# Three pieces of a gated macaron block's feed-forward stages put at other places: one split, one difference, one turning of a tile

## The chip, the cores and the metric

The kernel runs on one core of a Trainium2 chip. The metric is the device time of one execution in microseconds (us). Three timed runs of the kernel before gave 1066.24, 1067.35 and 1068.38 us; their median is 1067.35 us.

In the profile, PE is TensorE's matrix multiplication and PEld its loading of the stationary operand, DVE is VectorE, ACT is ScalarE, POOL is GpSimd, and SP is the engine that issues most of the DMAs.

## The reference, cut to what matters

One layer on 512 tokens of width 1024, all in float32:

```python
def rms_norm(x, g):
    return x * lax.rsqrt(jnp.mean(x * x, axis=-1, keepdims=True) + RMS_EPS) * g

def swiglu(h, w1, w3, w2):
    return (jax.nn.silu(h @ w1) * (h @ w3)) @ w2

x = x + 0.5 * swiglu(rms_norm(x, ffn1_norm), ffn1_w1, ffn1_w3, ffn1_w2)   # first FFN, inner width 2816
h = rms_norm(x, mix_norm); p = h @ w_in                                    # RWKV-7 and forgetting attention
x = x + (gate_a * y_a + gate_b * y_b) @ w_out                              # "the scan" and its projections
x = x + 0.5 * swiglu(rms_norm(x, ffn2_norm), ffn2_w1, ffn2_w3, ffn2_w2)    # second FFN
out = rms_norm(x, final_norm)
```

The change touches the two feed-forward stages (FFNs) alone; the mixers between them stay as they are.

## The kernel before, in words

**Every float32 product is three matmuls.** An operand is split into a rounded high part (`hi`) and the remainder (`lo = x - hi`), and hi·hi, hi·lo and lo·hi are added up in PSUM (`mm3`, lines 174 to 177; L175 to L177 in the profile, or L103 where the recorded queue below is in use). The high part is a cast by ACT, the low part a subtraction by DVE (`split`, `split_w`).

**Who sets the order.** From `written(True)` on, PE, DVE and ACT each run their instructions in the order in which the Python code names them (class `Queued`, lines 92 to 105: each call is issued behind the one before it on that engine). All of these instructions carry line 103 in the profile, so they are told apart by their tiles. Between engines only data counts: an instruction waits for what it reads and for the space it overwrites.

**The head of an FFN.** The first two feature tiles (128 of the 2816 inner features each) are done before the blocks, as plain products: `unit` multiplies a tile's split weights (`whi`, `wlo`) by the eight unnormalized input tiles, 24 matmuls, into the banks `pa` and `pb`. There are four such units: two weights (w1, w3) by two tiles. The weights of the fourth unit are split by `split_w(raws[3], KD, P)`. Meanwhile `normal` multiplies the eight input tiles in place by gain and 1/rms (tile `xS`, DVE); the blocks' sums and differences read these.

**The blocks.** The remaining 20 feature tiles of w1 and w3 are five blocks of four. A block takes seven products instead of eight (Strassen's scheme in Winograd's form), each of 24 matmuls into two banks. Class `Wide` lists the 35 products in `s.order` as (block, product): positions 0 to 3 are (0,0) (1,0) (0,6) (1,6), then come (0,1) (0,2) (0,4) (0,5) (1,1) (0,3) (1,2) (1,4) (1,5) (2,0) (1,3) and so on up to position 34. `blocks` walks this list: for each position and each of its two halves h it names the matmuls, at h = 1 the `finish` of the product (copies out of the banks, sums, gates), and after each half the split of the weights for the position two further on (`weight(m + 2, h)`).

A block's gate (silu of one product times another) leaves a tile `u` with tokens in the partitions, and the down projection needs features there. For early blocks a DMA does that turning: `apart` (two ACT copies of `u` into `p` or `sa`, as 16-bit words, and two transposing DMAs issued by SP) and later `joined` (four ACT copies from the turned words to the hidden tiles `rl` and `rh`). `joined` is entered in the table `joins` under the position at which it is to run. The last block's gate is turned by PE itself (`turn`: transposes `P<-ident,u`), behind steps 0, 2 and 3 of the next stage.

**The down projection.** Class `Seven` is seven products of 66 matmuls (11 steps k, two banks, three matmuls). `put(n, k, f, ...)` enters work behind step k of product n. `second`, `one` and `two` prepare its operands from the hidden tiles; `two(1)` is one subtraction of 128x1024 elements, written to the space of the old input tile (`xT<-rl` in the first FFN, `xS<-rl` in the second).

Of the kernel before, what the change touches and what calls it, by code (L numbers as in the profile page):

```python
# [19 lines left out]
P = 128  # L20
T = 512
D = 1024
KD = D // P
# [59 lines left out]
def kernel(  # L83
# [80 lines left out]
    def split_w(raw, kt, n, eng=None, hi_eng=None):  # L164
        hi = wp.tile([P, kt, n], F32R, tag="whi", name="whi", bufs=2)
        lo = wp.tile([P, kt, n], F32R, tag="wlo", name="wlo", bufs=2)
        (hi_eng or act).copy(hi[:], raw[:])  # L167
        (eng or dve).tensor_tensor(lo[:], raw[:], hi[:].bitcast(F32), op=ALU.subtract)  # L168
        return hi, lo
# [334 lines left out]
    class Seven:  # L504
# [65 lines left out]
        def run(s):  # L570
            tc.keep_in_program_order(act.preload_act_table_set("natural_log_exp_and_others"))
            X, Y, Z, V = s.banks

            def mm(ps, n, i, k, fresh, cols=slice(0, T)):
                qh, ql = [t[:, k % 4, i * P:(i + 1) * P] for t in s.q[n % 2][k // 4]]
                wh, wl = [t[:, k % 2, cols] for t in s.slots[k // 2]]
                stop = k == (9 if n == 6 else KH - 1)
                part = cols.stop - cols.start < T
                if part:
                    fresh = ps is Z  # L580
                else:
                    fresh, stop = fresh and k == 0, stop or n == 6 and k == 5
                return mm3(ps[i][:, cols], qh, ql, wh, wl, fresh and (not part or k == 8), stop, n in (2, 4, 5) or part and ps is V or n == 6 and k > 7)

            after = {}

            def put(n, k, *what):
                after.setdefault((n + k // KH, k % KH), []).append(what)

            put(0, 0, s.wide.turn, (1, 3), 0)  # L590
            put(0, 2, s.wide.turn, (0, 2), 1)
            put(0, 3, s.wide.turn, (1, 3), 1)
            put(0, 6, s.second, 2)
            put(0, 7, s.two, 2)
            for g, (two, four) in enumerate(((17, 25), (20, 28), (24, 31))):
                put(0, two, s.four, g)
                put(0, four, s.three, g)
            for n in range(6):
                for g in range(6):
                    put(n, min(2 * g + (5 if n == 0 else 3), 11 if n == 5 else 99), s.weight, n + 1, g)  # L600
                for g in range(3):
                    if n + 2 < 7:
                        put(n, min(4 * g + 3, 10) + (4 if n == 0 else 0), s.operand, n + 2, g)
            for n, ps in enumerate((X, Y, X, Z, Y, X)):
                for k in range(KH):
                    for i in range(2):
                        mm(ps, n, i, k, n in (0, 1, 3))
                    for f, *a in after.get((n, k), ()):
                        f(*a)
                for i in range(2):  # L610
                    for b, cols, by in (((0, LO, 0.5),), ((2, HI, 0.5),), ((0, HI, -0.5),), ((2, LO, 0.5),),
                                        ((0, HI, 0.5),), ((2, HI, -0.5), (2, LO, 0.5)))[n]:
                        s.out(ps[i][:], b + i, cols, by)
                if n == 0:
                    written(False)
                s.done(n)
            first_k, last_k = (0, 1, 2, 3, 6, 7, 10), (4, 5, 8, 9)
            for at, k in enumerate(first_k):
                for i in range(2):
                    s.mm = mm(V, 6, i, k, True)  # L620
                for f, *a in after.get((6, k), ()):
                    f(*a)
                s.between(at)
            for i in range(2):
                a, c = s.parts if i else (LO, None)
                for k in last_k:
                    s.mm = mm(V, 6, i, k, True, LO if c is None or k < 8 else a)
                    s.ending(i, k)
                s.out(V[i][:, a], i, a, 0.5)
                if c:  # L630
                    s.out(V[i][:, c], i, c, 0.5)
                    for k in last_k[2:]:
                        mm(Z, 6, i, k, k == 8, c)
                    s.out(Z[i][:, c], i, c, 0.5)
                    s.finished(i, a)
                s.finished(i, c or a)
# [13 lines left out]
    class Wide:  # L650
# [258 lines left out]
        def blocks(s, pa, pb, more):  # L909
# [12 lines left out]
                    (1, 2): ((s.low, 6),),  # L922
                    (2, 5): ((sv.second, 0),), (3, 2): ((sv.two, 0),),
                    (end, 0): ((sv.operand, 0, 0),), (end, 2): ((sv.operand, 0, 1),), (end, 6): ((sv.one, 0),),
                    (end, 5): ((sv.second, 1), (sv.one, 1)), (end, 4): ((sv.two, 1), *[(s.plain, sv.O[i], s.residual[i]) for i in range(2)])}
            for at, steps in more.items():
                todo[at] = tuple(todo.get(at, ())) + steps
            joins = {}
            for m, (b, n) in enumerate(s.order):
                apart = n == 4 and (b < EARLY or b == end)  # L930
                early = m < 2 * EARLY
                ps = s.X[b % 2] if n in (0, 2, 3, 5) or early else s.X[(b + 1) % 2] if n == 6 or apart else s.Y[b % 2]
                onto = n in (2, 3, 5) or (n == 6 and early) or (n == 4 and not apart)
                last = m + 2 >= len(s.order)
                if last:
                    sv.slots += s.ring[2 * m % 4:2 * m % 4 + 2]
                for h in range(2):
                    wh, wl = s.ring[(2 * m + h) % 4]
                    for i in range(2):
                        for k in range(2):  # L940
                            c = slice(i * P, (i + 1) * P)
                            if early:
                                qh, ql = [t[4 * (n > 0) + 2 * h + k][:, c] for t in raw]
                            else:
                                qh, ql = [t[:, 2 * h + k, c] for t in s.q[n]]
                            mm3(ps[i][:], qh, ql, wh[:, k], wl[:, k], not onto and h + k == 0, h + k == 2, onto)
                    if (b, n, h) == (end, 2, 0):
                        s.turn_half(b - 1)
                    if h == 1:
                        if m == len(s.order) - 1:  # L950
                            s.turns = dict(zip((0, 2, 1, 3), s.Y[end % 2] + s.X[1 - end % 2]))
                            act.activation(s.sa[0], ps[0][:], AF.Silu)
                            act.activation(s.sa[1], ps[1][:], AF.Silu)
                            s.turn((0, 2), 0)
                            for i in range(2):
                                dve.tensor_tensor(s.u[1][:, i], s.u[1][:, i], s.sa[i], op=ALU.mult)
                            sv.operand(0, 2)
                        else:
                            s.finish(m)
                    if h == 1:  # L960
                        for f, *a in soon.get((b, n), ()):
                            f(*a)
                    if not last:
                        s.weight(m + 2, h)
                    elif len(sv.slots) == 2:
                        sv.weight(0, h)
                    elif h == 0:
                        sv.slots.insert(2, s.last)
                        sv.weight(0, 2)
                        sv.weight(0, 3)  # L970
                    else:
                        sv.weight(0, 4)
                    if (m, h) in joins:
                        s.joined(*joins[m, h])
                    if b in (2, 3) and (n, h) == (1, 1):
                        s.apart(b - 1, 1)
                        joins[m + 3, 0] = b - 1, 1
                if n == 4 and b < end or (b, n) == (0, 3):
                    s.apart(b, int(n == 3))
                    joins[m + 3, 0] = b, int(n == 3)  # L980
                s.gate(m)
                for f, *a in todo.get((b, n), ()):
                    f(*a)
# [125 lines left out]
    with ExitStack() as mx:  # L1109
# [397 lines left out]
        at = b1.go(range(2))  # L1507
# [685 lines left out]
    with tc.tile_pool(name="hp", bufs=1) as hp:  # L2193
# [17 lines left out]
        wide.places()  # L2211
        wide.normal(range(2))
        wide.weight(0, 0)
        for m in range(2, KD):
            wide.unit(ps[1], ws[1], (m - 2,))
            wide.normal((m,))
        wide.unit(ps[1], ws[1], range(KD - 2, KD))
        pa, pb = bank("pa", pr), bank("pb", pf)
        ws.append(split_w(raws[3], KD, P))
        wide.unit(pa, ws[2])  # L2220
        wide.unit(pb, ws[3])
        wide.weight(0, 1)
# [30 lines left out]
```

## Time and profile before

| | |
|---|---|
| median of three runs | 1067.35 us (1066.24 to 1068.38) |
| the profiled execution's own time | 1067.36 us |
| its span, first to last instruction | 1065.7 us, granted TensorE clock 0.999 |
| PE busy | 1054.2 us, 99% of the span |
| first FFN, blocks | from about 32 to 224 us |
| second FFN, head / blocks / down projection | from about 738 / 760 / 952 us |

1067.36 - 1065.7 = 1.7 us lie outside the span. A matmul of 512 columns is shown as 0.39 us long, but matmuls overlap: they start about 0.227 us apart when nothing is waited for. So a wait of PE is read from the distance between two starts rather than from the "idle before" of a row. In the timeline a row is: start, duration, engine, line, operation, what it writes<-reads, shape and count, and in brackets the engine's idle time before it with what ended it; where "x2" or more stands, equal instructions that follow each other are merged and the duration is that of all of them.

### The profile page before, as it was taken

What the parts mean: (1) busy time and instruction counts of PE and PEld (TensorE: products, weight loads), DVE (VectorE), ACT (ScalarE), POOL (GpSimd) and SP (SyncE); (2) the same over time, 40 slices, a digit from 0 to 9 for tenths busy, and PEclk for the clock granted to TensorE, in tenths of its full rate; (3) what the DMA queues carried; (4) which work ended last, traced back from release to release, by engine and by line L of the source; (5) the groups of instructions that cost most, each with busy time, mean ns of one, the idle gap of its engine ahead of it and who ended that gap; (6) DMA issues with size and microseconds to landing.
All of it is one profiled execution on the core that took longest, in us unless ns stands there. A gap on an engine that the chain in (4) does not pass through costs nothing.

```text
span 1065.7 us, 16736 instructions
## 1 busy us (share of the span) xinstructions
PE 1054.2 (99%) x6178; PEld 862.5 (81%) x6178; DVE 841.4 (79%) x1171; ACT 712.4 (67%) x1107; POOL 242.4 (23%) x291
## 2 busy tenths in 40 slices
PE   9999999999999999999999999999999999999997
PEld 7888888888887887888777877888888888888886
DVE  7997776789865698878988878866698766699874
ACT  6777767776555766445888766544578868676554
POOL 1221220134203202312012230135311212114210
PEclk9999999999999999999999999999999999999999
DMA  7999999889946443443345574666989999979972
GB/s 215 262 193 233 230 196 253 201 194 189 230 125 170 116 112 97 129 132 106 85 82 117 130 186 154 196 160 166 282 199 212 208 229 231 212 205 202 235 187 80
DMA packets 194960, 190.25 MB, mean 179 GB/s; under 512 B 64958, under 2 KB 131070, under 8 KB 194878
## 3 DMA queue, kind: packets, MB, share of 16 engines
q1 hardware_dynamic: 147230, 110.78, 37.0%
q0 software_dynamic: 33392, 70.14, 34.8%
q10 hardware_dynamic: 14256, 8.26, 2.9%
q8 instruction: 49, 0.80, 0.3%
q14 instruction: 33, 0.27, 0.1%
HBM read 163.51 MB, written 12.52 MB: 165 GB/s over the span
## 4 chain that ended last, share of the span: by engine, by line
PE 88%; DVE 5%; ACT 3%; issue 2%; DMA 1%; SPq 1%; DVEq 0%; ACTq 0%
PE P L103 33%; PE P L177 6%; PE P L176 6%; PE P L175 6%; PE pgt L103 5%; PE spot L103 3%; PE pq L103 3%; PE l L103 2%; PE ppj L103 2%; PE pk L175 2%; PE pk L177 2%; PE pk L176 2%; PE pw L176 1%; PE pw L175 1%; PE pw L177 1%
## 5 line engine op out<-in xcount | busy, mean ns | idle before, releaser
L103 PE MATMUL P<-sraw,q 128*128 128x512 f32 x344 | 91.3, 389 | 0.0
L103 PEld LDWEIGHTS P<-sraw,q 128*128 128x128 f32 x344 | 64.6, 188 | 13.4
L103 PE MATMUL P<-swhi,q 128*128 128x512 f32 x224 | 71.2, 389 | 0.0
L167 ACT CAST whi<-raw 128x1024 fp32r<-128x1024 f32 (+2 forms) x42 | 40.4, 961 | 44.2 <-issue 14.1
L103 PE MATMUL P<-sraw,wxh 128*128 128x512 f32 x200 | 67.7, 390 | 0.0
L693 POOL DMA_DIRECT2D cb<-in_ffn_w_dram x20 | 24.1, 1207 | 143.3 <-DVE cd L103 76.2
L168 DVE TENSOR_TENSOR wlo<-raw,whi 128x1024 fp32r<-128x1024 f32 (+2 forms) x43 | 48.5, 1127 | 10.3 <-ACT whi L167 9.1
L103 PE MATMUL P<-swhi,wxh 128*128 128x512 f32 x144 | 56.6, 393 | 0.0
L103 PE MATMUL P<-swhi,wxl 128*128 128x512 f32 x144 | 56.1, 390 | 0.0
L103 PE MATMUL P<-swlo,wxh 128*128 128x512 f32 x144 | 56.1, 389 | 0.0
L693 POOL DMA_DIRECT2D cd<-in_ffn_w_dram x24 | 29.3, 1221 | 113.2 <-DVE sraw L103 59.7
L103 PE MATMUL P<-sraw,wxl 128*128 128x512 f32 x136 | 52.9, 389 | 0.0
L103 PEld LDWEIGHTS P<-swhi,q 128*128 128x128 f32 x224 | 42.0, 188 | 8.8
L103 ACT COPY RD<-spot 32x128 f32<-32x128 f32 (+2 forms) x128 | 39.9, 312 | 10.8 <-PE spot L103 8.8
L103 DVE TENSOR_TENSOR u<-P,u 128x512 f32<-128x512 f32 x52 | 33.4, 683 | 13.7 <-ACT u L103 13.7
L103 PEld LDWEIGHTS P<-sraw,wxh 128*128 128x128 f32 x200 | 37.5, 188 | 7.7
L103 PE MATMUL P<-swlo,q 128*128 128x512 f32 x112 | 43.6, 389 | 0.0
L552 POOL DMA_DIRECT2D ca<-in_ffn_w_dram x16 | 19.3, 1205 | 95.0 <-DVE swlo L103 65.6
L177 PE MATMUL pk<-xh,wlo 128*128 128x512 f32 x96 | 37.5, 392 | 1.0 <-DVE wlo L168 1.0
L175 PE MATMUL pk<-xh,whi 128*128 128x512 f32 x96 | 38.0, 396 | 0.4 <-DVE u L1257 0.4
L176 PE MATMUL pk<-xl,whi 128*128 128x512 f32 x96 | 37.5, 390 | 0.0
L177 PE MATMUL P<-swhi,wxl 128*128 128x512 f32 x96 | 37.3, 389 | 0.0
(632 smaller groups left out, 3441.9 us busy)
## 6 DMA issues: line engine op xcount, KB each, us to landing
cc<-in_ffn_w_dram SPq DMA_DIRECT2D x36, 512.0 KB
cb<-in_ffn_w_dram POOLq DMA_DIRECT2D x36, 512.0 KB, 6.6
cb<-in_ffn_w_dram SPq DMA_DIRECT2D x32, 512.0 KB
cd<-in_ffn_w_dram POOLq DMA_DIRECT2D x32, 512.0 KB, 8.1
ca<-in_ffn_w_dram POOLq DMA_DIRECT2D x32, 512.0 KB, 8.6
raw<-in_w_in_dram SPq DMA_DIRECT2D x27, 512.0 KB
ca<-in_ffn_w_dram SPq DMA_DIRECT2D x20, 512.0 KB
cd<-in_ffn_w_dram SPq DMA_DIRECT2D x18, 512.0 KB
```

The costliest lines, as they stand in the source:

```text
L103: q.last = do(*a, **kw)
L167: (hi_eng or act).copy(hi[:], raw[:])
L168: (eng or dve).tensor_tensor(lo[:], raw[:], hi[:].bitcast(F32), op=ALU.subtract)
L175: pe.matmul(ps, whi, xhi, start=first, stop=False, skip_group_check=onto)
L176: pe.matmul(ps, whi, xlo, start=False, stop=False, skip_group_check=onto)
L177: return pe.matmul(ps, wlo, xhi, start=False, stop=last, skip_group_check=onto)
L552: nc.gpsimd.dma_start(s.sum[g], src, accum_op=ALU.add)
L693: nc.gpsimd.dma_start(to, s.block(b, n, h), accum_op=ALU.add)
```

## The change

Three pieces move; no instruction is added or removed.

1. In both FFNs, the turning of block 0's first gate half, `apart(0, 0)`, moves from behind product (0,4) (position 6) to the middle of (0,5) (position 7), behind that half's `weight`. The `joined(0, 0)` that belongs to it moves from the middle of position 9 to the middle of position 10.
2. In both FFNs, `two(1)` moves from behind product (4,4), the last but one, to behind step 5 of the down projection's first product.
3. In the second FFN's head, the split of the fourth unit's weights moves ahead of the normalization of input tiles 2 to 7. The interleaving of `unit` and `normal` in the code goes too; as PE and DVE each keep their own order, that changes nothing on PE.

```diff
@@ Seven.run
             put(0, 3, s.wide.turn, (1, 3), 1)
+            put(0, 5, s.two, 1)
             put(0, 6, s.second, 2)
@@ Wide.blocks
-                    (end, 5): ((sv.second, 1), (sv.one, 1)), (end, 4): ((sv.two, 1), *[(s.plain, sv.O[i], s.residual[i]) for i in range(2)])}
+                    (end, 5): ((sv.second, 1), (sv.one, 1)), (end, 4): [(s.plain, sv.O[i], s.residual[i]) for i in range(2)]}
...
                     if (m, h) in joins:
                         s.joined(*joins[m, h])
+                    if m > 0 and (s.order[m - 1], h) == ((0, 4), 0):
+                        s.apart(0, 0)
+                        joins[m + 3, 0] = 0, 0
...
-                if n == 4 and b < end or (b, n) == (0, 3):
+                if n == 4 and 0 < b < end or (b, n) == (0, 3):
                     s.apart(b, int(n == 3))
                     joins[m + 3, 0] = b, int(n == 3)
@@ the second FFN
         wide.normal(range(2))
         wide.weight(0, 0)
-        for m in range(2, KD):
-            wide.unit(ps[1], ws[1], (m - 2,))
-            wide.normal((m,))
-        wide.unit(ps[1], ws[1], range(KD - 2, KD))
+        wide.unit(ps[1], ws[1])
+        ws.append(split_w(raws[3], KD, P))
+        wide.normal(range(2, KD))
         pa, pb = bank("pa", pr), bank("pb", pf)
-        ws.append(split_w(raws[3], KD, P))
         wide.unit(pa, ws[2])
         wide.unit(pb, ws[3])
```

On the engines this reads as follows. The order of PE's and SP's instructions is the same before and after; POOL's differs in one place of the second FFN's head, where a DMA issue and two copies change places.

DVE at the second FFN's head, before (`xS` with `rstd`: the normalizations; `wlo<-raw,whi`: splits of unit weights; `sraw`, `extra`, `swlo`: splits for the first block products):

```order
L103 TENSOR_TENSOR wlo<-raw,whi 128x1024 x2
L103 SCALAR_TENSOR_TENSOR xS_6333<-xS_6333,par,rstd 128x512 x2
L103 TENSOR_TENSOR sraw<-cd_6889,sraw 128x1024
L103 SCALAR_TENSOR_TENSOR xS_6333<-xS_6333,par,rstd 128x512 x2
L103 SCALAR_TENSOR_TENSOR xS_6334<-xS_6334,par,rstd 128x512 x4
L103 TENSOR_TENSOR wlo<-raw,whi 128x1024
L103 TENSOR_TENSOR extra<-cd_6890,sraw 128x1024
```

and now:

```order
L103 TENSOR_TENSOR wlo<-raw,whi 128x1024 x2
L103 SCALAR_TENSOR_TENSOR xS_6333<-xS_6333,par,rstd 128x512 x2
L103 TENSOR_TENSOR sraw<-cd_6889,sraw 128x1024
L103 TENSOR_TENSOR wlo<-raw,whi 128x1024
L103 SCALAR_TENSOR_TENSOR xS_6333<-xS_6333,par,rstd 128x512 x2
L103 SCALAR_TENSOR_TENSOR xS_6334<-xS_6334,par,rstd 128x512 x4
L103 TENSOR_TENSOR extra<-cd_6890,sraw 128x1024
```

The last `wlo` went from behind six normalizations to ahead of them.

DVE where the second FFN's blocks end and its down projection begins, before (`xS<-rl` is `two(1)`; `u<-u,sa` is the last block's gate, which PE turns; the others are splits):

```order
L103 TENSOR_TENSOR swlo<-ca_6888,swhi 128x1024
L103 TENSOR_TENSOR xS_6333<-rl_6882 128x1024
L103 TENSOR_TENSOR q_6899<-cb_6891,q_6899 128x1024
L103 TENSOR_TENSOR sraw<-cb_6892,sraw 128x1024
L103 TENSOR_TENSOR u_6897<-u_6897,sa_6974 128x512
L103 TENSOR_TENSOR u_6897<-u_6897,sa_6975 128x512
L103 TENSOR_TENSOR wxl_7118<-rl_6883,wxh_7117 128x768
L103 TENSOR_TENSOR extra<-cd_6889,sraw 128x1024
L103 TENSOR_TENSOR g_8401<-cd_6890,g_8400 128x512
L103 TENSOR_TENSOR swlo<-ca_6887,swhi 128x1024
```

and now:

```order
L103 TENSOR_TENSOR swlo<-ca_6888,swhi 128x1024
L103 TENSOR_TENSOR q_6899<-cb_6891,q_6899 128x1024
L103 TENSOR_TENSOR sraw<-cb_6892,sraw 128x1024
L103 TENSOR_TENSOR u_6897<-u_6897,sa_6974 128x512
L103 TENSOR_TENSOR u_6897<-u_6897,sa_6975 128x512
L103 TENSOR_TENSOR wxl_7118<-rl_6883,wxh_7117 128x768
L103 TENSOR_TENSOR extra<-cd_6889,sraw 128x1024
L103 TENSOR_TENSOR g_8400<-cd_6890,g_8399 128x512
L103 TENSOR_TENSOR xS_6333<-rl_6882 128x1024
L103 TENSOR_TENSOR swlo<-ca_6887,swhi 128x1024
```

`two(1)` went seven rows down; the two gate rows each stand one row higher. The first FFN has the same rows with `xT` for `xS`.

ACT from the middle of product (0,3) (position 9) to that of (1,2) (position 10) in the second FFN, before (`rl<-u`, `rh<-u`: the four copies of `joined(0, 0)`; `sa<-P`: the silu of (0,3); `sa<-u`: the copies of `apart(0, 1)`; the last two rows are the copies out of the banks of (1,2)):

```order
L103 COPY rl_6881<-u_6896 128x512
L103 COPY rh_6884<-u_6896 128x512
L103 COPY rl_6881<-u_6896 128x512
L103 COPY rh_6884<-u_6896 128x512
L103 ACTIVATE sa_6974<-P_7099 128x512
L103 ACTIVATE sa_6975<-P_7100 128x512
L103 CAST swhi<-cc_6894 128x1024
L103 COPY sa_6974<-u_6897 128x1024
L103 COPY sa_6975<-u_6897 128x1024
L103 CAST wxh_7117<-xS_6334 128x1024
L103 CAST sraw<-cb_6891 128x1024
L103 COPY u_6896<-P_7101 128x512
```

and now:

```order
L103 ACTIVATE sa_6974<-P_7099 128x512
L103 ACTIVATE sa_6975<-P_7100 128x512
L103 CAST swhi<-cc_6894 128x1024
L103 COPY sa_6974<-u_6897 128x1024
L103 COPY sa_6975<-u_6897 128x1024
L103 CAST wxh_7117<-xS_6334 128x1024
L103 CAST sraw<-cb_6891 128x1024
L103 COPY rl_6881<-u_6896 128x512
L103 COPY rh_6884<-u_6896 128x512
L103 COPY rl_6881<-u_6896 128x512
L103 COPY rh_6884<-u_6896 128x512
L103 COPY u_6896<-P_7101 128x512
```

The four copies went from ahead of the silu of (0,3) to just ahead of the copies out of the banks of (1,2). Earlier in the same list the two copies `p<-u` of `apart(0, 0)` changed places with one cast, `swhi<-cd`, and the first FFN's ACT list has the same moves.

More of the change, by code (lines that the diff above doesn't have):

```diff
@@ L924, in blocks @@
                     (end, 0): ((sv.operand, 0, 0),), (end, 2): ((sv.operand, 0, 1),), (end, 6): ((sv.one, 0),),
-                    (end, 5): ((sv.second, 1), (sv.one, 1)), (end, 4): ((sv.two, 1), *[(s.plain, sv.O[i], s.residual[i]) for i in range(2)])}
+                    (end, 5): ((sv.second, 1), (sv.one, 1)), (end, 4): [(s.plain, sv.O[i], s.residual[i]) for i in range(2)]}
             for at, steps in more.items():
-                todo[at] = tuple(todo.get(at, ())) + steps
+                todo[at] = tuple(todo.get(at, ())) + tuple(steps)
             joins = {}
```

## The prediction

> **What bounds the kernel now.** I read the page's busy times first, then busy time by stretch, then the chain of waits, and last the timeline around each edit.
>
> ```profile
> PE 1054.2 (99%) x6178; PEld 862.5 (81%) x6178; DVE 841.4 (79%) x1171; ACT 712.4 (67%) x1107; POOL 242.4 (23%) x291
> PE 88%; DVE 5%; ACT 3%; issue 2%; DMA 1%; SPq 1%; DVEq 0%; ACTq 0%
> core 0: us, PE busy (x) PEld busy (x) DVE busy (x) ACT busy (x) POOL busy (x), PEclk, DMA share, GB/s
> 65.20:114.10 48.90, 48.90 (x217) 40.52 (x216) 40.59 (x44) 38.49 (x50) 8.47 (x7) 1.00 0.99 223
> 793.30:842.20 48.90, 48.90 (x217) 40.51 (x216) 40.25 (x44) 38.54 (x50) 8.47 (x7) 1.00 0.99 221
> ```
>
> PE is the bound: 99% of the span, 88% of the chain. The two stretches are block positions 6 to 14 of the first and of the second FFN, where the first edit lies: nine products, 216 matmuls in 48.90 us, 0.226 us from start to start, with PE busy in all of the time. So there is no wait of PE to remove there, and one product takes 48.90 / 9 = 5.43 us. Whatever the change gains has to be a wait of PE elsewhere. The chain shows where DVE work of the moved kind stands ahead of PE:
>
> ```profile
> 754.06 1.15 DVE wlo L103
> 755.25 5.29 PE pb L103 x22
> ...
> 952.92 1.15 DVE xS L103
> ...
> 956.25 1.29 DVE u L103 x2
> 957.58 11.95 PE P L103 x55
> ```
>
> PE's fourth unit waits for the last weights' split (third edit), and PE's turning waits for a gate that stands behind `two(1)` on DVE (second edit).
>
> **Third edit, the head of the second FFN.** PE, then DVE, then ACT:
>
> ```profile
> 754.62 0.39 PE L103 MATMUL pb<-xl,whi 128*128 128x512 f32 x1
> 755.25 0.50 PE L103 MATMUL pb<-xh,wlo 128*128 128x512 f32 x1 [0.24 <-DVE wlo L103]
> ...
> 755.82 0.40 PE L103 MATMUL pb<-xl,whi 128*128 128x512 f32 x1
> ```
>
> ```profile
> 750.00 4.06 DVE L103 SCALAR_TENSOR_TENSOR xS<-xS,par,rstd 128x512 f32<-128x512 f32 x6
> 753.97 1.22 DVE L103 TENSOR_TENSOR wlo<-raw,whi 128x1024 fp32r<-128x1024 f32 x1
> 756.31 1.23 DVE L103 TENSOR_TENSOR extra<-cd,sraw 128x1024 fp32r<-128x1024 f32 x1 [1.12 <-ACT sraw L103]
> ...
> 765.78 1.22 DVE L103 TENSOR_TENSOR rl<-xS,xS 128x1024 f32<-128x1024 f32 x1
> ```
>
> ```profile
> 748.92 1.06 ACT L103 CAST whi<-raw 128x1024 fp32r<-128x1024 f32 x1 [0.16 <-PE pb L103]
> 755.23 1.05 ACT L103 CAST sraw<-cd 128x1024 fp32r<-128x1024 f32 x1 [5.25 <-DVE wlo L103]
> ```
>
> From 754.62 to 755.82 are three steps, 1.20 us where 3 x 0.227 = 0.68 would do: PE loses 0.52 us. The split's high part is ready at 748.92 + 1.06 = 749.98, which is when the six normalizations start at 750.00. Put first, the split ends at about 750.00 + 1.22 = 751.2, and its matmul would come at 754.62 + 0.23 = 754.85: 3.6 us of cover, the wait goes whole. Now the six normalizations are late, by one split's spacing, 1.14 us. Their first reader is the difference `rl<-xS,xS` at 765.78; they end at 755.2, so 10 us cover them. The second split of the first block weights (`extra`) waited for ACT, and ACT for the raw tile that `wlo` reads; both come some 1.1 us earlier or at the same time. Gain 0.52 us; the bounds are 0 (the wait passes to something equally late, of which I see none) and 0.52, since PE loses no more there.
>
> **Second edit, both FFNs.** PE's third turning, with the undisturbed second turning ahead of it as the measure; then the first FFN's; then DVE, and the gate's silu on ACT:
>
> ```profile
> 953.54 0.39 PE L103 MATMUL P<-swhi,wxl 128*128 128x512 f32 x1
> 953.77 0.60 PE L103 MATMUL P<-ident,u 128*128 128x128 f32 x4
> 954.13 0.48 PE L103 MATMUL P<-swhi,wxh 128*128 128x512 f32 x1
> ...
> 956.73 0.39 PE L103 MATMUL P<-swhi,wxl 128*128 128x512 f32 x1
> 957.07 0.30 PE L103 MATMUL P<-ident,u 128*128 128x128 f32 x1
> 957.58 0.55 PE L103 MATMUL P<-ident,u 128*128 128x128 f32 x3 [0.21 <-DVE u L103]
> 957.89 0.48 PE L103 MATMUL P<-swhi,wxh 128*128 128x512 f32 x1
> ```
>
> ```profile
> 228.77 0.39 PE L103 MATMUL P<-swhi,wxl 128*128 128x512 f32 x1
> ...
> 229.91 0.48 PE L103 MATMUL P<-swhi,wxh 128*128 128x512 f32 x1
> ```
>
> ```profile
> 952.84 1.22 DVE L103 TENSOR_TENSOR xS<-rl 128x1024 f32<-128x1024 f32 x1
> 953.98 1.22 DVE L103 TENSOR_TENSOR q<-cb,q 128x1024 fp32r<-128x1024 f32 x1
> ...
> 956.25 1.28 DVE L103 TENSOR_TENSOR u<-u,sa 128x512 f32<-128x512 f32 x2
> ...
> 959.46 0.68 DVE L103 TENSOR_TENSOR g<-cd,g 128x512 fp32r<-128x512 f32 x1
> 961.41 1.22 DVE L103 TENSOR_TENSOR swlo<-ca,swhi 128x1024 fp32r<-128x1024 f32 x1 [1.27 <-ACT swhi L103]
> ```
>
> ```profile
> 952.14 0.60 ACT L103 ACTIVATE sa<-P 128x512 f32<-128x512 f32 x1 [0.77 <-PE P L103]
> ```
>
> Undisturbed, the four transposes take 954.13 - 953.54 = 0.59 us from the matmul before to the one behind; here 957.89 - 956.73 = 1.16, in the first FFN 229.91 - 228.77 = 1.14. PE loses 0.57 and 0.55 us. DVE goes without a gap from 952.84 on, so without `two(1)` all up to `g` moves up by 953.98 - 952.84 = 1.14 us. The gate's two products then end at 957.53 - 1.14 = 956.39, where PE wants the first at 956.73 + 0.23 = 956.96. That leaves 0.57 us, and the next thing they wait for, ACT's silu, ended at 952.74. Both waits go whole. `two(1)` itself now follows `g` and ends at 960.14, just when `g` ended before; behind it `swlo<-ca` waits for ACT until 961.41, so 1.27 us of idle DVE cover even a late one. Without that cover it would cost a split 1.14 us, whose reader is the second product of the stage, 66 x 0.227 = 15 us after the first one's start: nothing. Gain 0.57 + 0.55 = 1.12 us, bounds 0 and 1.12.
>
> **First edit, both FFNs.** The copies of `apart(0, 0)` change places with one cast; what they free or feed has the rest of the way to position 10. Its two transposing DMAs are issued about a cast later, 1 us, and SP, which takes its list in order, issues the block weights behind them later by as much. These belong to position 13 and are split at position 11, about three products (3 x 5.43 = 16 us) behind their issue in position 8; I cost that at nothing, and without that cover at 1 us, the cast's. The four copies of `joined` are what can hurt:
>
> ```profile
> 812.50 1.05 ACT L103 CAST swhi<-cc 128x1024 fp32r<-128x1024 f32 x1 [1.62 <-PE P L103]
> 813.46 0.68 ACT L103 COPY rl<-u 128x512 uint16<-128x512 uint16 x1
> ...
> 815.78 1.07 ACT L103 ACTIVATE sa<-P 128x512 f32<-128x512 f32 x2
> ...
> 821.48 1.06 ACT L103 COPY u<-P 128x512 f32<-128x512 f32 x2
> ...
> 834.57 1.08 ACT L103 COPY u<-P 128x512 f32<-128x512 f32 x2
> ```
>
> ```profile
> 836.78 0.62 PE L103 MATMUL P<-sraw,q 128*128 128x512 f32 x2
> ```
>
> They take 815.78 - 813.46 = 2.32 us. Taken out ahead of the silu, ACT gets there at 813.5, but that product's second bank is complete only near 836.78 - 4 x 5.43 = 815.06, so ACT can use about half of the time: the silus would end near 815.7 instead of 816.85, and everything up to the copies moves up by 1.15. Behind the four copies, `u<-P` at 821.48 is then 2.32 - 1.15 = 1.2 us late. `joined` reads the space that `u<-P` overwrites, on the same engine, in order. Behind `u<-P` on ACT are the casts for the next products; DVE waits for it with `u<-P,u`, and ACT later for DVE's gate, so the 1.2 us can travel to `u<-P` at 834.57. The first of these two copies ends near 835.1, and position 14, which adds onto the same banks, starts at 836.78: 1.7 us in hand, 1.2 in the second FFN, where PE comes 0.52 us earlier. Lateness 1.2 against 1.7 and 1.2: I take a cost of 0, between 0 and the slower rival's price below. A gain here is excluded by the 48.90 of 48.90.
>
> **Sum.** The profiled execution took 1067.36 us (span 1065.7 and 1.7 around it), as good as the median of 1067.35. 1067.36 - 0.52 - 0.57 - 0.55 = 1065.72, so **1065.7 us**, 0.15% faster. About 0.2% of this kernel, 2.1 us, is what a measurement can tell from no change; the three runs alone lie 2.1 us apart. By that measure the likeliest outcome is "same".
>
> **Rivals.** (a) The first FFN's 0.55 us is lost in the scan, or one of the waits stays in part: 1067.36 - 0.52 - 0.57 = 1066.3. For it: 12% of the chain is not PE, and stands mostly in the scan. Against it: those are chains between instructions, which all start earlier together; transfers, which could keep to a time of their own, are 1% of the chain.
>
> (b) PE has room, and makes up for its small waits, so nothing reaches the end: 1067.4. PE's weight loading is busy 81% only. The Trainium skill, "Perfetto Trace Analysis", Identifying the Most-Contended Engine, says that matmul busy time tells little on the distance to the best possible and that weight-loading busy time tells more; taken so, 19% would be room, and waits of 1.6 us could vanish in it. The trace speaks against making up: 216 starts in 48.90 us, the same in both FFNs, so after a wait PE goes on at its pace, not faster.
>
> (c) The slower side: the four copies stay whole on ACT's path to the banks of position 14. If none of the 2.32 us is won back, and the copy behind them waits for the last one's full 0.68 instead of its spacing of 0.58, the first copy at 834.57 ends at 835.1 + 2.42 = 837.5: PE waits 0.75 us in the first FFN's counterpart of 836.78 and 0.75 + 0.52 = 1.27 in the second. That is 2.0 against a gain of 1.64: 1065.72 + 2.02 = 1067.7. It decides from a lateness of 1.2 us on, which is what I reckon, so it is near. For it: DVE and ACT are busy 40 and 38.5 of 48.90 us there. Against it: ACT has 10 us of idle in that stretch.
>
> **Chances and range.** Forecast 0.60; (a) 0.17; (b) 0.06; (c) 0.11; something faster than counted, 0.06. The range is 1064.3 to 1067.8: from 1.4 us below the forecast, the scatter of a median whose runs lie 2.1 us apart, to (c). The border of "faster" is 1067.35 x 0.998 = 1065.2, only 0.5 us below the forecast; I give it a third of the forecast's 0.60 and most of the last case, together 0.25. "Slower" begins at 1069.5, above every case: 0.05. Same: 0.70.
>
> **What would show it.** Right: in the head, `pb` matmuls 0.227 us apart without a wait for `wlo`; four transposes `P<-ident,u` merged behind step 2 of both down projections, as at 953.77; 48.90 of 48.90 again for positions 6 to 14; and, against the profile before, a scan that begins 0.55 us earlier and block products of the second FFN that begin 0.55 + 0.52 = 1.07 us earlier. Wrong: a wait of PE for ACT `u` near position 14, for DVE `u` as before, or a scan that ends at the old time although the first FFN ended earlier.

## The result, and the profile after

| | kernel before | changed kernel |
|---|---|---|
| median (runs) | 1067.34 us (22) | 1065.72 us (22) |
| range of the runs | 1066.24 to 1068.48 | 1064.61 to 1066.67 |
| ratio, 95% interval | | 0.9984, 0.9977 to 0.9991 |
| profiled execution: own time, span | 1067.36, 1065.7 us | 1066.64, 1064.9 us |

The changed kernel is 0.16% faster, and the interval excludes no change; it is still less than the 0.2% that the prediction called a difference. Of the profiled executions, the changed kernel's is near the upper end of its runs, and the two lie only 0.72 us apart. Most of this section and the next is about that number: why a single pair of profiles shows 0.72 us where the medians show 1.62. The ratios, here and below, are not quotients of the medians, and two slow runs, of 6052.6 us (kernel before, timed with experiment 1) and of 1507.04 us (third edit alone), are left out of them.

The busy times and the chain of waits of the changed kernel:

```profile
PE 1054.1 (99%) x6178; PEld 863.2 (81%) x6178; DVE 842.8 (79%) x1171; ACT 712.0 (67%) x1107; POOL 243.4 (23%) x291
PE 92%; DVE 4%; DMA 1%; ACT 1%; issue 1%; SPq 0%; DVEq 0%; ACTq 0%; POOL 0%; POOLq 0%
```

The busy times are those of before; PE's share of the chain rose from 88% to 92%, since the chain no longer leaves PE for DVE at the moved places. The chain of waits of the changed kernel, cut to the second FFN (start, duration, what, number of matmuls), has PE alone:

```profile
743.99 5.48 PE pb L103 x24
749.47 5.44 PE pa L103 x24
754.90 5.44 PE pb L103 x24
...
760.57 204.56 PE P L103 x914
```

A unit of 24 matmuls takes 24 x 0.227 = 5.45 us, and the fourth one, the last `pb`, takes 5.44 now; behind it 204.56 us of PE follow, up to 965 us where the view ends, without one step on another engine. DVE's part of it, from the timeline:

```profile
750.36 1.22 DVE L103 TENSOR_TENSOR wlo<-raw,whi 128x1024 fp32r<-128x1024 f32 x1
751.50 4.06 DVE L103 SCALAR_TENSOR_TENSOR xS<-xS,par,rstd 128x512 f32<-128x512 f32 x6
755.48 1.22 DVE L103 TENSOR_TENSOR extra<-cd,sraw 128x1024 fp32r<-128x1024 f32 x1
...
954.91 1.28 DVE L103 TENSOR_TENSOR u<-u,sa 128x512 f32<-128x512 f32 x2
...
958.12 0.68 DVE L103 TENSOR_TENSOR g<-cd,g 128x512 fp32r<-128x512 f32 x1
958.73 1.21 DVE L103 TENSOR_TENSOR xS<-rl 128x1024 f32<-128x1024 f32 x1
```

The split of the last unit's weights stands ahead of the six normalizations and ends at 751.58, 3.3 us before the unit starts; `two(1)` (`xS<-rl`) stands behind `g`. PE's turning of the last gate, in the second and in the first FFN:

```profile
956.54 0.39 PE L103 MATMUL P<-swhi,wxl 128*128 128x512 f32 x1
956.77 0.60 PE L103 MATMUL P<-ident,u 128*128 128x128 f32 x4
957.13 0.48 PE L103 MATMUL P<-swhi,wxh 128*128 128x512 f32 x1
```

```profile
229.10 0.39 PE L103 MATMUL P<-swhi,wxl 128*128 128x512 f32 x1
229.34 0.60 PE L103 MATMUL P<-ident,u 128*128 128x128 f32 x4
229.69 0.48 PE L103 MATMUL P<-swhi,wxh 128*128 128x512 f32 x1
```

The four transposes are one row, and from the matmul ahead to the one behind it is 0.59 us at both places: the undisturbed value.

**Where the time went.** Every matmul of one kernel has its counterpart in the other, so the starts of the same matmul in two profiles can be subtracted. I give these differences as steps between two fixed places, with the profile of before as the measure (us, negative is earlier); the experiments' kernels stand below the change, as they belong to one table. "Start" is all that comes before 33 us, "82" is block position 9 of the first FFN, "111" its positions 12 to 14, "810" position 9 of the second FFN, and with it, for the kernel of experiment 5, positions 12 to 14. "230" and "957" are the turnings, "755" is the fourth unit of the head, and "465" and "585" lie in the scan.

```
                                start   82   111   230    465    585    755   810   957 |  end
the change                      +0.27 +0.05 +0.02 -0.56  +1.10  -0.55  -0.53  0.00 -0.56 | -0.78
second edit alone               -0.20 +0.02 +0.02 -0.55  -0.18  -0.40  -0.01  0.00 -0.57 | -1.92
third edit alone                -0.28 +0.14 +0.02 +0.04  +0.25  -0.38  -0.53  0.00 +0.01 | -0.79
first edit alone                -0.30 +0.01 +0.01 +0.02  +1.37  -0.39  -0.13  0.00 +0.01 | +0.62
second and third                +0.34 +0.82 +0.02 -0.56  +0.88  -0.08  -0.53  0.00 -0.56 | +0.30
DVE late, without first edit    +0.31 +1.74 -0.02 -0.56  +0.23  -0.50  -0.53 +2.33 -0.56 | +2.34
DVE late, with first edit       -0.21 +1.36 +0.02 -0.56  -0.18  -0.46  -0.53 +1.21 -0.56 | -0.02
joined twice                    +0.39  0.00 +2.43 -0.56  -0.11  -0.61  -0.53 +2.40 -0.56 | +2.81
half of two(1) in old place     -0.30  0.00 +0.03 -0.52  +0.62  -0.35  -0.53  0.00 -0.53 | -1.63
split behind five               -0.21  0.00 +0.02 -0.56  -0.18  -0.55  -0.53  0.00 -0.56 | -2.66
```

In the first row the three predicted steps are there: 0.56 at 230 us (0.55 predicted), 0.53 at 755 (0.52), 0.56 at 957 (0.57), 1.65 together. The other columns of that row are not the edits' work: the start was 0.27 us later, the scan lost 1.10 us at one place and won 0.55 at another. Pairs of rows show it. The kernel "split behind five" has the same code as the change up to the head of the second FFN, and still a start of -0.21 and a step of -0.18 at 465 us. The kernels were not all run on the same chip, but "second edit alone" and "second and third" were; they have the same code up to that head too, and differ by 0.54 us at the start, by 0.80 at 82 us and by 1.06 at 465. Such differences explain why the ends lie 0.78 us apart and not 1.65.

### The profile page after: what moved, and what is told of

Read it like the earlier page. It is cut to its first block, busy times and chain, and to the rows that moved or that the text cites. A ratio compares the mean times of both kernels' runs of the same rounds, so it can differ in the third digit from the quotient of the medians.

```text
span 1064.9 us, 16739 instructions
## 1 busy us (share of the span) xinstructions
PE 1054.1 (99%) x6178; PEld 863.2 (81%) x6178; DVE 842.8 (79%) x1171; ACT 712.0 (67%) x1107; POOL 243.4 (23%) x291
## 4 chain that ended last, share of the span: by engine, by line
PE 92%; DVE 4%; DMA 1%; ACT 1%; issue 1%; SPq 0%; DVEq 0%; ACTq 0%; POOL 0%; POOLq 0%
PE P L103 39%; PE P L177 6%; PE P L176 6%; PE P L175 6%; PE pgt L103 5%; PE spot L103 3%; PE pq L103 3%; PE l L103 2%; PE ppj L103 2%; PE pb L103 2%; PE pa L103 2%; PE pk L175 1%; PE pk L176 1%; PE pw L176 1%; PE pk L177 1%; PE pw L177 1%
```

## Experiment 1: the edits one by one

Four kernels made of the kernel before, timed together with it. The edits are the hunks of the diff above:

```diff
 second edit alone
+            put(0, 5, s.two, 1)
-                    ... (end, 4): ((sv.two, 1), *[(s.plain, sv.O[i], ...
+                    ... (end, 4): [(s.plain, sv.O[i], ...
 third edit alone
+        wide.unit(ps[1], ws[1])
+        ws.append(split_w(raws[3], KD, P))
+        wide.normal(range(2, KD))
 first edit alone
+                    if m > 0 and (s.order[m - 1], h) == ((0, 4), 0):
+                        s.apart(0, 0)
+                        joins[m + 3, 0] = 0, 0
-                if n == 4 and b < end or (b, n) == (0, 3):
+                if n == 4 and 0 < b < end or (b, n) == (0, 3):
```

> The kernel before with the second edit alone: the 128x1024 subtraction of two(1) behind step 5 of the down projection's first product, in both FFNs. My theory: PE's starts behind the turning move 0.55 us earlier in the first FFN (about 230 us) and a further 0.57 us in the second (about 958 us), neither is lost again in the scan, and the time falls by about 1.1 us, to some 1066.2 us beside 1067.3 us. The rival that the scan takes the first FFN's part back: only the second step shows at the end, 0.57 us, 1066.8 us. The rival that PE makes up small waits: no change at the end.

> The kernel before with the third edit alone: the fourth unit's weights split ahead of the six normalizations. My theory: one step of PE's starts, 0.52 us earlier from about 755 us on, nothing at any other place that does not also vary between runs of the kernel before; 1066.8 us beside 1067.3 us. The rival that PE makes up small waits: 0.52 us at 755 us that is gone again by the end, no change.

> The kernel before with the first edit alone: block 0's first gate half parted and joined one product later, in both FFNs. My theory: 0.0 us, with a lateness of 1.2 us that PE does not see, so 1067.3 us and 48.90 of 48.90 us busy in block positions 6 to 14. The rival that the four joined copies stand whole on ACT's path: PE waits 0.75 us in the first FFN and 1.27 us in the second near position 14, so 2.0 us slower, 1069.4 us.

> The second and the third edit without the first. My theory: the same as the whole change, three steps of 0.55, 0.52 and 0.57 us, 1.64 us faster than before, 1065.7 us. If the first edit costs PE something that the whole change hides, this kernel is faster than the whole change by that, at least 0.2 us; if the first edit brings something in the presence of the others (a rival that I gave little), it is slower than the whole change.

Measured, beside 1067.89 us of the kernel before (median of 33 runs):

| | median us (runs) | ratio, 95% interval |
|---|---|---|
| second edit alone | 1066.40 (11) | 0.9986, 0.9977 to 0.9994 |
| third edit alone | 1067.25 (11) | 0.9991, 0.9982 to 1.0000 |
| first edit alone | 1067.63 (11) | 1.0000, 0.9991 to 1.0010 |
| second and third | 1066.38 (11) | 0.9987, 0.9978 to 0.9996 |

Against the kernel before the medians are 1.49, 0.64, 0.26 and 1.51 us lower, where 1.1, 0.5, 0 and 1.6 were expected; the intervals, 1.8 to 2.0 us wide, can't tell more than that. The traces can. The second and the third edit do what was predicted at their own places and nothing at the others' places: 0.55 and 0.57 us for the second, 0.53 for the third. In the second FFN the waits of PE say the same; first the kernel with the second edit alone, then the one with the third alone (engine and tile waited for, us, times, longest):

```profile
PE pb L103 <- DVE wlo L103: 0.2, 1, 0.2
```

```profile
PE P L103 <- DVE u L103: 0.2, 1, 0.2
```

One wait is left in each, the one that the other edit removes. The change itself has none there.

**Rival (a), the scan.** The second edit alone settles whether the first FFN's 0.55 us is lost again: the offset is the same from 230 to 462 us (its drift there is 0.02 us). What happens at 465 us is another thing. DVE waits there for a DMA, and PE for a split that stands behind this work on DVE. The wait's row in five kernels: before, the change, the second edit alone, the first edit alone, and the kernel "split behind five", whose code up to here is that of the change:

```profile
458.80 0.19 DVE L1405 TENSOR_TENSOR prod<-TT,Ls 128x31 f32<-128x31 f32 x1 [4.23 <-DMA Ls<-Ld]
```

```profile
459.66 0.19 DVE L1409 TENSOR_TENSOR prod<-TT,Ls 128x31 f32<-128x31 f32 x1 [5.30 <-DMA Ls<-Ld]
463.63 0.50 PE L176 MATMUL pv<-wlo,xh 128*128 128x512 f32 x1 [0.94 <-DVE wlo L168]
```

```profile
457.52 0.19 DVE L1406 TENSOR_TENSOR prod<-TT,Ls 128x31 f32<-128x31 f32 x1 [3.67 <-DMA Ls<-Ld]
```

```profile
459.92 0.19 DVE L1408 TENSOR_TENSOR prod<-TT,Ls 128x31 f32<-128x31 f32 x1 [5.57 <-DMA Ls<-Ld]
```

```profile
457.45 0.19 DVE L1409 TENSOR_TENSOR prod<-TT,Ls 128x31 f32<-128x31 f32 x1 [3.67 <-DMA Ls<-Ld]
```

DVE's idle time there was 4.23, 5.30, 3.67, 5.57 and 3.67 us, and PE's step 0, +1.10, -0.18, +1.37 and -0.18: PE loses what DVE's wait for that DMA is longer than 4.23 us. From its issue to its landing the DMA took 4.4, 5.1, 4.1, 5.1 and 3.8 us. In all eleven profiles the idle time lies between 3.46 and 5.57 us and the step follows it to within 0.07 us, down to a floor of -0.18. It does not depend on how late the kernel comes to the scan: the two kernels that came latest, 1.4 and 2.3 us behind before, had 4.44 and 4.11 us. Rival (a) would need a scan that gives back what the first FFN won; here it gives and takes up to 1.5 us for a reason of its own.

**The first edit.** Its kernel has no step at 82 us or 111 us, as predicted. But the kernel *without* it, the second and third edits, lost 0.82 us at 82 us, where the profile of before shows 48.90 of 48.90 us busy, and where the second edit alone, with the same code up to there, lost 0.02. DVE and PE there (`q<-xT,q` is the input half that position 9 reads; it ends at 82.93):

```profile
82.06 0.39 PE L103 MATMUL P<-swlo,q 128*128 128x512 f32 x1
82.98 0.73 PE L103 MATMUL P<-swhi,q 128*128 128x512 f32 x2 [0.53 <-DVE q L103]
```

```profile
69.61 1.22 DVE L103 TENSOR_TENSOR sraw<-ca,sraw 128x1024 fp32r<-128x1024 f32 x1
72.45 1.23 DVE L103 TENSOR_TENSOR ca<-ca,cb 128x1024 f32<-128x1024 f32 x1 [1.62 <-DMA cb<-in_ffn_w_dram]
...
77.77 1.22 DVE L103 TENSOR_TENSOR ca<-ca,cb 128x1024 f32<-128x1024 f32 x1
79.37 1.23 DVE L103 TENSOR_TENSOR swlo<-cd,swhi 128x1024 fp32r<-128x1024 f32 x1 [0.37 <-ACT swhi L103]
80.51 1.28 DVE L103 TENSOR_TENSOR u<-P,u 128x512 f32<-128x512 f32 x2
81.71 1.22 DVE L103 TENSOR_TENSOR q<-xT,q 128x1024 fp32r<-128x1024 f32 x1
```

The chain begins with a load: DVE's first `ca<-ca,cb` waits for weights (`cb`). In before the same rows are these:

```profile
69.28 1.22 DVE L103 TENSOR_TENSOR sraw<-ca,sraw 128x1024 fp32r<-128x1024 f32 x1
71.10 1.23 DVE L103 TENSOR_TENSOR ca<-ca,cb 128x1024 f32<-128x1024 f32 x1 [0.60 <-DMA cb<-in_ffn_w_dram]
...
78.00 1.22 DVE L103 TENSOR_TENSOR swlo<-cd,swhi 128x1024 fp32r<-128x1024 f32 x1 [0.35 <-ACT swhi L103]
```

From `sraw` to `ca` it is 1.82 us in before and 2.84 here: the weights came 1.0 us later, and without the first edit DVE then also waits 0.37 us for a cast, `swhi<-cd`, which ACT does behind the two long copies of `apart`; in before that wait was there too, 0.35 us. In the changed kernel the cast stands ahead of the copies:

```profile
76.01 1.05 ACT L103 CAST swhi<-cd 128x1024 fp32r<-128x1024 f32 x1
76.96 1.99 ACT L103 COPY p<-u 128x1024 uint16<-128x1024 uint16 x2
```

and DVE's `swlo<-cd,swhi` no longer waits for it. That made a new theory: the first edit costs nothing and gains nothing while the weights are early, as in the profile of before, and takes 0.4 to 0.5 us off PE's wait when they are late.

## Experiment 2: the weights late on purpose, with and without the first edit

Two kernels, the second and third edits alone and the whole change. In both, two more subtractions that write what is already there stand ahead of `ca<-ca,cb`, so that it is late by a known time:

```diff
@@ Wide.weight
+            if (b, n, h) == (1, 1, 0):
+                for _ in range(2):
+                    hi, lo = s.ring[(2 * m + h) % 4]
+                    dve.tensor_tensor(lo, here, f32(hi), op=ALU.subtract)
             if n == 1:
                 dve.tensor_tensor(here, here, s.B[h], op=ALU.add)
```

> The second and third edits without the first, and on DVE two idle repeats of a 128x1024 subtraction (sraw<-ca,sraw, about 1.14 us each, the result the same) ahead of ca<-ca,cb in both FFNs, so that this instruction is about 1.6 us later than in the profile before, as it is when its weights land late. My new theory, that the first edit buys room for such lateness (in the four kernels so far PE lost 0.82 us where ca<-ca,cb came 1.0 us late without the edit, and 0.05 where it came 0.7 us late with it): PE waits about 1.4 us at position 9 of the first FFN (about 82 us) and 1.3 us at that of the second (about 811 us), against the kernel without the repeats, some 2 us slower than before less the 1.6 us of the other edits: 1068.3 us where before takes 1067.4. The rival, that the wait of 0.82 us was another jitter that has nothing to do with DVE's lateness: no wait here, 1065.9 us.

> The whole change with the same two repeats. My new theory: the first edit takes the two part copies (p<-u, 1.9 us on ACT) out from ahead of the cast swhi<-cd, for which DVE waited 0.35 us, and so buys about 0.45 us at each of the two places: PE waits about 0.95 us at 82 us and 0.85 us at 811 us, 0.9 us less in all than the kernel without the first edit, 1067.4 us. The rival, that the first edit is nothing but a reordering of ACT without an effect on PE: the same waits as without it.

DVE and PE, first without the edit, then with it:

```profile
69.59 3.73 DVE L103 TENSOR_TENSOR sraw<-ca,sraw 128x1024 fp32r<-128x1024 f32 x3
73.36 1.23 DVE L103 TENSOR_TENSOR ca<-ca,cb 128x1024 f32<-128x1024 f32 x1
...
83.87 0.73 PE L103 MATMUL P<-swhi,q 128*128 128x512 f32 x2 [1.45 <-DVE q L103]
```

```profile
69.07 3.73 DVE L103 TENSOR_TENSOR sraw<-ca,sraw 128x1024 fp32r<-128x1024 f32 x3
72.84 1.23 DVE L103 TENSOR_TENSOR ca<-ca,cb 128x1024 f32<-128x1024 f32 x1
...
82.91 0.74 PE L103 MATMUL P<-swhi,q 128*128 128x512 f32 x2 [1.02 <-DVE q L103]
```

With the same 3.77 us from `sraw` to `ca`, PE lost 1.74 us without the edit and 1.36 with it (column "82"). Expected were 1.4 and 0.95: both waits are longer than that, but the edit takes off 0.38 us where 0.45 was expected. The rival for the first of the two, a jitter unrelated to DVE, and the rival for the second, no effect on PE, both fall. These are one profile each; what makes them more than that is that all eleven profiles follow one rule: the loss at 82 us against the time from `sraw` to `ca`.

```
without the first edit   1.82 1.97 2.15 2.84 3.77      with it   2.05 2.16 2.24 2.41 2.54 3.77
PE's loss, us            0.00 0.02 0.14 0.82 1.74                0.00 0.01 0.00 0.00 0.05 1.36
```

Without the edit the loss is the time beyond 2.02 us, with it the time beyond some 2.41 to 2.49: the edit buys about 0.4 us. Over the nine profiles without the added subtractions, the rule gives a mean loss of 0.25 us without the edit (the excess over 2.02) and 0.05 with it (over 2.45). So it is worth about 0.2 us on average in the first FFN; that is an estimate from nine executions, it takes for granted that the edit doesn't change when the weights come, and it is less than the timed runs can tell (first edit alone: 0.9991 to 1.0010). In the second FFN these weights are early, none of the nine lost anything at 810 us, and the edit brings nothing there. With the repeats, the kernel without the edit lost 2.33 us there and the other 1.21, where 1.3 and 0.85 were expected. Of this difference of 1.12 us, 0.67 are no effect of the edit: measured from PE's starts, DVE came to the three subtractions that much later in the one execution than in the other. What remains is 0.45 us, but the place is no clean measure.

The medians were 1069.71 us without (7 runs; ratio 1.0028, 1.0016 to 1.0040) and 1069.16 with the edit (10 runs; 1.0029, 1.0008 to 1.0050), 1067.50 before. Both lie above what was expected, 1068.3 and 1067.4. The second one's runs reach from 1067.28 to 1076.12, and its profiled execution, 1067.32, is nearly the fastest of them, so the times do not separate the two; only the traces do. In part my expectation was too low since the repeats cost more: three subtractions on the same tiles took 3.73 us, where I had counted 1.14 us each beside the first.

## Experiment 3: the copies of `joined` twice

To measure how near rival (c) was, each of the four copies that the first edit moves is done twice in the changed kernel:

```diff
-        def joined(s, b, half):
+        def joined(s, b, half, again=1):
-            for f in range(4):
+            for f in [f for f in range(4) for _ in range(again)]:
...
-                        s.joined(*joins[m, h])
+                        s.joined(*joins[m, h], 2 if joins[m, h] == (0, 0) else 1)
```

> The whole change with each of the four joined(0,0) copies done twice, so 2.32 us more of ACT behind position 10. My theory, by which ACT's lateness of 1.2 us at u<-P is covered by 1.7 us in hand (first FFN) and 1.2 us (second): PE waits 1.2 + 2.3 - 1.7 = 1.8 us near position 14 of the first FFN and 1.2 + 2.3 - 1.2 = 2.3 us in the second, 4.1 us in all, 1069.8 us. The rival that the copies never were on PE's path, with far more cover than I counted: no wait, 1065.8 us. If the slack I read is too large by half a microsecond, each wait is that much longer.

Median 1071.11 us (5 runs) beside 1067.50 before, ratio 1.0037 (1.0024 to 1.0050). ACT behind position 10 of the second FFN, in the changed kernel and with the copies doubled, and then PE in the latter:

```profile
820.26 0.69 ACT L103 COPY rl<-u 128x512 uint16<-128x512 uint16 x1
...
822.72 1.08 ACT L103 COPY u<-P 128x512 f32<-128x512 f32 x2
...
835.40 1.08 ACT L103 COPY u<-P 128x512 f32<-128x512 f32 x2
```

```profile
821.45 1.40 ACT L103 COPY rl<-u 128x512 uint16<-128x512 uint16 x2
...
826.75 1.07 ACT L103 COPY u<-P 128x512 f32<-128x512 f32 x2
```

```profile
827.39 0.74 PE L103 MATMUL P<-sraw,wxh 128*128 128x512 f32 x2 [0.32 <-ACT u L103]
840.06 2.11 PE L103 MATMUL P<-sraw,q 128*128 128x512 f32 x8 [1.29 <-ACT u L103]
```

PE waits for `u<-P`, at position 12 already and again at 14, and loses 2.43 us in the first FFN and 2.40 in the second, 4.83 in all where 4.1 was expected. The doubled copies cost 826.75 - 821.45 - (822.72 - 820.26) = 2.84 us and not 2.32. So of the added 2.84 us PE lost 2.4 in both: in the changed kernel 0.4 us are still in hand. `u<-P` stands 1.43 us later in it than in before (822.72 + 0.19 - 821.48, with the offset of PE's starts), so 1.43 + 0.43 = 1.9 us were in hand before, counted at this copy. Not all of the lateness travels on: at the later `u<-P`, the one that position 14 needs, it is 835.40 + 0.19 - 834.57 = 1.02 us, and 1.02 + 0.43 = 1.45 us were in hand there. I had counted that the 1.2 us would travel whole, against 1.7 in the first FFN and 1.2 in the second. The rival of no wait at all is excluded. Rival (c) had the right mechanism, and its place, but decides from 1.9 us of lateness at the first copy on, not from 1.2.

## Experiment 4: what cover is left at the other two edits

Half of `two(1)` back ahead of the gate, the other half behind step 5; and, in the head, the split behind five of the six normalizations:

```diff
+            put(0, 5, s.less, 1, 2, 4)
-            put(0, 5, s.two, 1)
...
+                    ... (end, 4): [(sv.less, 1, 0, 2)] + [(s.plain, ...
```

```diff
         wide.unit(ps[1], ws[1])
+        wide.normal(range(2, 7))
         ws.append(split_w(raws[3], KD, P))
-        wide.normal(range(2, KD))
+        wide.normal(range(7, KD))
```

(`less(1, k0, k1)` is `two(1)` on the column parts k0 to k1 of four.)

> The whole change with two of the four column parts of two(1) (128x512 elements, 0.6 us) back at the old place ahead of the gate, and the other half behind step 5. My theory: the whole of two(1) made PE wait 0.55 and 0.57 us with 1.14 us of DVE ahead of the gate, so the cover left is 0.57 us and half of it costs 0 to 0.1 us in each FFN: 1065.7 to 1065.9 us, four transposes P<-ident,u close together. The rival that the gate is bound by something else (ACT's silu) and the difference only adds to it: a wait that is half of the old, 0.28 us in each FFN, 1066.3 us.

> The whole change, but the fourth unit's weights split behind five of the six normalizations of the second FFN's head, not ahead of all six. My theory, that only DVE's order held PE up and that there is cover of 3.6 us: the five take 5 x 0.68 = 3.4 us of it, so the split ends about 0.2 us ahead of its matmul, no wait at 755 us, and the end as in the whole change. The rival that the split has other waits behind it (a bank, the high part): a wait of up to 0.5 us that is there already with five, as it was with six.

The half costs 0.04 us in the first FFN and 0.03 in the second, beside 0.56 for the whole (columns "230" and "957"). The timed runs, 1066.24 us in the median of 10, ratio 0.9995 (0.9979 to 1.0012), scatter too much to say more. DVE and PE in the second FFN:

```profile
951.73 0.68 DVE L103 TENSOR_TENSOR xS<-rl 128x512 f32<-128x512 f32 x1
952.34 1.22 DVE L103 TENSOR_TENSOR q<-cb,q 128x1024 fp32r<-128x1024 f32 x1
...
954.61 1.28 DVE L103 TENSOR_TENSOR u<-u,sa 128x512 f32<-128x512 f32 x2
...
955.87 0.63 PE L103 MATMUL P<-ident,u 128*128 128x128 f32 x4
```

The half puts 0.61 us of DVE work (951.73 to 952.34) ahead of the gate and costs 0.04; 1.14 us cost 0.56. Both give a cover of 0.57 or 0.58 us, as the prediction had it, and the rival of a proportional cost (0.28) is out. PE starts the turning at 955.87, and the gate's two products end at 954.61 + 1.28 = 955.89. In before, too, the first of the four transposes ran ahead and only the other three waited for the second product; here that product comes just when they are due, and nothing is left in hand.

With the split behind five normalizations PE loses nothing at 755 us: the split ends at 751.63 + 1.22 = 752.85 in that profile, and the matmul that wants it starts at 753.32:

```profile
748.32 3.40 DVE L103 SCALAR_TENSOR_TENSOR xS<-xS,par,rstd 128x512 f32<-128x512 f32 x5
751.63 1.22 DVE L103 TENSOR_TENSOR wlo<-raw,whi 128x1024 fp32r<-128x1024 f32 x1
...
753.32 0.39 PE L103 MATMUL pb<-xh,wlo 128*128 128x512 f32 x1
```

So five of the six could have stayed in front, and the wait came from DVE's order alone. This kernel's single run, 1064.77 us beside one of 1068.29 of before, is no proof of a better kernel: its scan had one of the earliest DMAs (step -0.18 against the +1.10 of the change's profile).

## Why the prediction was right, and where it was not

**Third edit, 0.52 us.** Measured 0.53 in every kernel that has it. The cover was sufficient by far: five normalizations of it can be given back. The profile of the first edit alone shows what else is in this figure: its wait was 0.13 us shorter, so the gain is 0.4 to 0.5 us, depending on the execution.

**Second edit, 0.55 and 0.57 us.** Measured 0.55 to 0.57 at both places wherever the whole of `two(1)` was moved. The 0.57 us of cover, worked out from the end of the gate and PE's wish for it, is confirmed by the half that costs 0.04.

**First edit, 0.** Right for a pair of profiles in which the weights come early, and wrong as a statement on the kernel. The step that failed is "A gain here is excluded by the 48.90 of 48.90": that is one execution's row. In another execution of the same order PE waited 0.82 us in that very stretch, since a load ended 1.0 us later. The change's own profile has 48.90 of 48.90 again, in both FFNs. The sum lacks a term of about 0.2 us, by the estimate of experiment 2. With it 1.84 us would have been forecast; the measured ratio's interval, 1.0 to 2.5 us, holds 1.64 and 1.84 alike. The row that should have warned was DVE's wait of 0.60 us for `cb`, with a wait for ACT, `swhi`, behind it: both stand on the way to `q<-xT,q`.

**Lateness behind `joined`, 1.2 us against 1.7 and 1.2.** Measured 1.4 against 1.9 in both, counted at the first `u<-P`, or 1.0 against some 1.4 at the second, where the prediction counted. So the verdict, no wait, was right, and two figures were not. ACT takes back 0.4 us between the two copies. And the second FFN's smaller figure was a mistake: PE is earlier there by the head's 0.52 us, but ACT's work ahead waits for PE's products, so ACT is earlier by the same. A gain ahead of a stage moves the stage as a whole and takes nothing from the slack within it. For the same reason rival (c)'s 0.52 us extra was not there.

**Rival (a)** fell: 0.55 us at 230 us is still there at 462, and what the scan does is a DMA's affair. My argument against it, that transfers are only 1% of the chain, was beside the point: that transfer's lateness moved PE by up to 1.5 us.

**Rival (b)** fell: no profile shows PE making up a wait. All steps that the edits caused are whole at the end of the trace, with PEld busy 81% before and after. By the Trainium skill, "Perfetto Trace Analysis", Identifying the Most-Contended Engine, weight-loading busy time tells more of the room than matmul busy time; in this trace the 19% of free weight loading were no room in which a wait could vanish.

**Sum.** 1067.36 - 1.64 = 1065.7 was predicted, 1065.72 measured, 1.62 us under the kernel before. As single profiles scatter by more than 1 us at the start and in the scan, the agreement to 0.02 us is partly luck; the three steps in the traces are what confirms the working. One sign that the prediction named can't be read from a single pair of profiles: block products of the second FFN that begin 1.07 us earlier. They began 0.19 us earlier, since the start and the scan took the rest.

## What to carry to other kernels

A wait of PE that DVE's or ACT's order causes is read well from one profile: the distance between two starts, and when the work would end without the piece in front. A *missing* wait is not: where an engine waits for a DMA somewhere ahead of PE's operand, ask how much later the DMA may come before PE stops, since the next execution will try it. And where an edit is worth less than the runs scatter, compare the starts of the same instruction in two traces place by place, and test a supposed reserve by filling it on purpose.

## What the runs showed of the hardware

- A DMA's end varies between executions of the same code by nearly as much as the whole change is worth: DVE's wait for `Ls` in the scan was 3.67 and 5.11 us in two kernels that do not differ up to there and ran on the same chip (second edit alone, second and third), and 3.46 to 5.57 us in eleven profiles; the time until `cb` was there was 1.97 and 2.84 us in those two, and 1.82 to 2.84 in nine. From 60 to 72 us, ahead of that wait for `cb`, the DMA engines were 0.89 to 0.94 busy in these nine. The Trainium skill, "DMA: Bandwidth & Descriptors", Latency and other measured facts, says that HBM's access latency grows from 0.2 us to 2 us under high load. A spread of 1.0 us with the DMA engines some nine tenths busy is of that size, but no run here separates it from waiting in the queue.
- The same copy of 128x512 elements as 16-bit words took 0.58 us from start to start where four followed each other into different places, and 0.71 us where it was done again into the same place (821.45 to 822.16 in experiment 3). Three subtractions of 128x1024 elements on the same tiles took 3.73 us, 1.24 to 1.26 from one start to the next, where neighbours on different tiles are 1.14 us apart. I had not expected a repeat to cost more than its neighbour, and no run shows why it does.
